# Dilated-attention mixer: the merge factors and the merge of a head pair moved to later visits, the fill of the last visit spread

## The chip, the cores and the metric

One core of one Trainium2 chip runs the whole program. The metric is the device time of one execution in microseconds (us), the median of 3 runs. All arithmetic is in 32-bit floats; products whose precision matters are made of three TensorE multiplications, with each operand split into a high and a low part.

## What is computed

A two-layer encoder on 512 tokens of width 1024. Each layer is a token mixer, a cross-attention into 256 memory tokens and a gated MLP, each followed by a residual and a layer norm. Layer 0 mixes by differential attention, layer 1 by dilated sliding-window attention. Only the mixer of layer 1 is touched:

```python
def dilated_attention(x, w_qkv, w_o):
    qkv = (x @ w_qkv).reshape(B, S, G, 3, H, E)          # G = 3 groups, H = 16 heads, E = 64
    for g, (window, dilation) in enumerate(((128, 1), (512, 4), (2048, 16))):
        o, l = dilated_group(qkv[:, :, g, 0], qkv[:, :, g, 1], qkv[:, :, g, 2], window, dilation, slopes)
        outs.append(o); lses.append(l)                   # output and log softmax denominator
    wts = softmax(stack(lses), axis=0)
    o = sum(wts[..., None] * stack(outs), axis=0)        # the merge
    return o.reshape(B, S, D) @ w_o
```

## The kernel before

**Pairs and visits.** `dil_attention` (line 643) works on 8 head pairs p = 0 to 7, each in two halves v = 0 and 1 of the queries. Its `main` (line 802) goes through visits i = 0 to 16. Visit i makes the scores of half i (pair i // 2, v = i % 2; line 713), turns the exponentials of half i - 1 by TensorE transposes in four sets k = 0 to 3 (line 767), and multiplies them with the values (`values`, line 772). So pair 6 is scored in visits 12 and 13 and has its values in visits 13 and 14; pair 7 is scored in visits 14 and 15 and has its values in visits 15 and 16; visit 16 scores nothing.

**One visit on the engines.** TensorE's 24 score matmuls fill four PSUM banks. VectorE adds the bias and finds the maximum (line 722, two instructions for each of four `u` tiles), ScalarE takes the exponential (line 724). A set of four transposes goes into one of two PSUM banks `ps_t` and is copied out into `PT` by line 769: sets 0 and 2 by VectorE (copy 0 and copy 2 below), sets 1 and 3 by ScalarE. `u` has four buffers: the scores of visit i write into the buffers that the turns of visit i set free. Set 2 needs the bank of set 0, so it waits for copy 0; the values wait for copies 2 and 3. At the end of `values` the result is copied out of PSUM into the tiles `O` (lines 786 to 790).

**Factors and merge.** The three groups of a pair are merged by their softmax denominators. `factors(p)` (line 731), called at the end of the scores of v = 1, sends the statistics through DRAM to change their layout (lines 737 to 741, POOL's DMA queue, into tile `x0`), works out the factors in nine small VectorE instructions and one on ScalarE (lines 747 to 756), and sends them through DRAM again, spread over the partitions, into tile `F` (lines 757 and 761, POOL's queue; one buffer). The merge, at the end of `values(p, 1)`, multiplies and adds the two `O` tiles (one buffer each) with `F` (lines 792 to 794, VectorE) and splits the sum into a high part (`o1h`, line 218, ScalarE) and a low part (`o1l`, line 219, VectorE) of the mixer's output, K-tile p of the product with `w_o`.

**What sets the order.** TensorE runs its instructions in the order in which they are written. VectorE, ScalarE and the DMA queues get theirs from a scheduler when the program is built: among the instructions that it holds to be ready, by its own estimate of times, the one written earlier goes first. Once built, each queue is strictly in order. `issue_after(ins)` puts an instruction somewhere behind `ins` in the queue of the same engine; it doesn't say how far behind.

**Fill.** `weave` (line 287) lets TensorE work on something else between the steps of a visit. Up to visit 13 that is the projection of the next pair (31 or 62 us of multiplications for two visits). For visits 14 to 16 only `on_.early(0)` is left: 12 triples of multiplications (a triple: lines 239, 240, 241) of the product with `w_o`, which need the K-tiles 0 to 5. `late = on_.early(1)` is another 12 triples; `take(late, t)` runs triples of it until t ns are used up, by 648 ns each. The code before takes 3 triples at the start of visit 16, 3 ahead of its values, and the remaining 6 behind them. Then `OutNorm.finish` (line 356) runs 8 triples of K-tiles 0 to 3 for the row blocks 2 and 3, and after these the triples of K-tiles 6 and 7, for row block 0 first. Their weights are loaded as `raw` and split into `whi` and `wlo` (lines 218 and 219).

Of the kernel before, what the change touches and what calls it, by code (L numbers as in the profile page):

```python
# [9 lines left out]
F32 = mybir.dt.float32  # L10
# [3 lines left out]
ALU = mybir.AluOpType  # L14
# [3 lines left out]
SEQ = 512  # L18
# [129 lines left out]
def encoder(ctx: ExitStack, tc: tile.TileContext, wall, xin, lam, subln, conv, lngb, tabf, tabd, eye, out):  # L148
    nc = tc.nc
# [130 lines left out]
    def take(gen, t):  # L280
        while t > 0:
            d = next(gen, None)
            if d is None:
                break
            t -= d
# [357 lines left out]
    def dil_attention(act, oT, pools, vp, ap, on_, led):  # L643
        tab = vp.tile([128, 768], F32, name="tabd")
        nc.scalar.dma_start(tab, tabd)
        NP = LH // 2
        qk, v0, v12, st0, st12, O = {}, {}, {}, {}, {}, {}


        def keys(x, b):  # L650
# [50 lines left out]
        def scores(p, v):  # L701
            (q0, k0, q1, k1, q2, k2) = qk[p]
            if v == 0:
                st0[p] = ap.tile([128, 4, 4], F32, tag="st0", name="st0")
                st12[p] = ap.tile([128, 4, 4], F32, tag="st12", name="st12")
            bs = 2 * v, 2 * v + 1
            Ss = {(b, c): psS.tile([128, 512], F32, tag="s", name="S") for b in bs for c in range(2)}
            for b in bs:
                for q_, k_, f in ((q0, keys(k0, b), slice(0, 256)), (q1, k1[:, b, :], slice(256, 384)),
                                  (q2, k2[:, b, :], slice(384, 512))):  # L710
                    for c in range(2):
                        h = sl(c, 64)
                        nc.tensor.matmul(Ss[b, c][:, f], q_[h, b, :], k_[h], start=True, stop=True)  # L713
            us = []
            for (b, c), S in Ss.items():
                u = ap.tile([128, 512], F32, tag="u", name="u", bufs=4)
                slope = 2.0 ** (-(2 * p + c + 1) / 2.0)
                for n, s in enumerate((st0[p], st12[p])):
                    f = sl(n, 256)
                    t = tab[:, 512:768] if n else tab[:, sl(b // 3, 256)]  # L720
                    m = s[:, b, 2 * c:2 * c + 1]
                    nc.vector.tensor_tensor_reduce(out=u[:, f], in0=S[:, f], in1=t, scale=-slope,  # L722
                                                   scalar=3.0e38, op0=ALU.add, op1=ALU.min, accum_out=m)
                    nc.scalar.activation(u[:, f], u[:, f], AF.Exp, bias=m, scale=-1.0,  # L724
                                         accum_out=s[:, b, 2 * c + 1:2 * c + 2])
                us.append(u)
            if v == 1:
                O[p] = [ap.tile([128, 512], F32, tag=f"O{n}", name="O", bufs=1) for n in range(2)], factors(p)
            return us

        def factors(p):

            eng = nc.gpsimd
            sd = dram.tile([SEQ, 4], F32, name=f"sd{p}")
            fd = dram.tile([2, 2, SEQ], F32, name=f"fd{p}")
            a, b = st0.pop(p), st12.pop(p)
            eng.dma_start(sd[64:448, :].rearrange("(b p) k -> p b k", p=128), a[:, 0:3, :])
            eng.dma_start(sd[448:512, :], a[0:64, 3, :])
            eng.dma_start(sd[0:64, :], a[64:128, 3, :])
            x = ap.tile([128, 4, 4], F32, tag="x0", name="x0")  # L740
            eng.dma_start(x, sd.rearrange("(k r) c -> k r c", r=4))

            ms = [t.rearrange("p r (c k) -> p k c r", k=2) for t in (x, b)]
            w = ap.tile([128, 2, 2, 4], F32, tag="w0", name="w0")
            e = ap.tile([128, 2, 2, 4], F32, tag="w1", name="w1")
            z = ap.tile([128, 2, 4], F32, tag="w2", name="w2")
            nc.vector.tensor_tensor(z, ms[0][:, 0], ms[1][:, 0], op=ALU.min)
            for n in range(2):
                nc.vector.tensor_tensor(w[:, :, n], z, ms[n][:, 0], op=ALU.subtract)
            nc.scalar.activation(e, w, AF.Exp)  # L750
            for n in range(2):
                nc.vector.tensor_tensor(w[:, :, n], e[:, :, n], ms[n][:, 1], op=ALU.mult)
            nc.vector.tensor_tensor(z, w[:, :, 0], w[:, :, 1], op=ALU.add)
            nc.vector.reciprocal(z, z)
            for n in range(2):
                nc.vector.tensor_tensor(w[:, :, n], e[:, :, n], z, op=ALU.mult)
            eng.dma_start(fd.rearrange("c s (k r) -> k c s r", r=4), w)
            F = ap.tile([128, 2, 512], F32, tag="F", name="F", bufs=1)
            for c in range(2):
                f = fd[c]  # L760
                eng.dma_start(F[sl(c, 64)], bass.AP(f.tensor, f.offset, [[0, 64], [SEQ, 2], [1, SEQ]]))
            return F

        def turn(u, n):
            tp = bank(pt, "t").rearrange("p (a b) -> p a b", b=128)
            for k in range(4):
                nc.tensor.transpose(tp[:, k, :], u[:, sl(k)], ident)  # L767
            PT = ap.tile([128, 4, 128], F32, tag="PT", name="PT", bufs=4)
            (nc.scalar.copy if n % 2 else nc.vector.tensor_copy)(PT, tp)
            return PT  # L770

        def values(p, v, PTs):
            o = bank(pt, "t")
            for x in range(2):
                b = 2 * v + x
                for n in range(4):
                    for c in range(2):
                        if n < 2:
                            V = v0[p // 2][b + n if b < 3 else 3 * n][:, (p % 2) * 128 + c * 64:]
                        else:  # L780
                            V = v12[p // 2][b][:, (p % 2) * 256 + (n - 2) * 128 + c * 64:]
                        nc.tensor.matmul(o[sl(c, 64), sl(2 * (n // 2) + x)], V[:, :64], PTs[2 * x + c][:, n, :],  # L782
                                         start=n % 2 == 0, stop=n % 2 == 1)
            (o0, o12), F = O[p]
            if v == 0:
                nc.scalar.copy(o0[:, 64:320], o[:, 0:256])
            else:
                nc.scalar.copy(o0[:, 320:512], o[:, 0:192])
                nc.scalar.copy(o0[:, 0:64], o[:, 192:256])
            nc.vector.tensor_copy(classes(o12)[:, sl(v, 2), :], o[:, 256:512].rearrange("p (r k) -> p r k", r=2))  # L790
            if v == 1:
                nc.vector.tensor_tensor(o0, o0, F[:, 0], op=ALU.mult)
                nc.vector.tensor_tensor(o12, o12, F[:, 1], op=ALU.mult)
                nc.vector.tensor_tensor(o0, o0, o12, op=ALU.add)
                evac(o0, oT[0][:, p, :], oT[1][:, p, :])

        def two_banks():
            return [psS.tile([128, 512], F32, tag="s", name="S") for _ in range(2)]
# [3 lines left out]
        def main():  # L802
            n = 2 * NP
            us = {}
            for i in range(n + 1):
                seg, step = (i // 2, 1 / 2.0) if i < n - 2 else (NP - 1, 1 / 3.0)
                pos = seg + (i - 2 * seg) * step
                yield pos
                if i < n:
                    us[i] = scores(i // 2, i % 2)  # L810
                else:
                    take(late, 1300)
                if i > 0:
                    PTs = []
                    for k in range(4):
                        yield pos + TURNS[k] * step
                        PTs.append(turn(us[i - 1][k], k))
                    yield pos + VALUES * step
                    if i == n:
                        take(late, 1300)  # L820
                    values((i - 1) // 2, (i - 1) % 2, PTs)

        run(proj(0))
        weave(main(), [(proj(p + 1), 6 * 5184 + 31104 * (p % 2)) for p in range(NP - 1)]
# [124 lines left out]
    for l in range(2):  # L949
        mt_kv = mems[l]  # L950
        oT = new_act(f"o{l}")
# [107 lines left out]
```

## Time and profile before

| what | us |
|---|---|
| median of 3 runs | 1894.35 |
| the three runs | 1894.87, 1894.35, 1891.37 |
| the profiled execution, its own time | 1890.71 |
| its span from first to last instruction | 1888.9 |
| TensorE busy in the span | 1863.5 (99%) |
| VectorE busy | 951.3 (50%) |
| ScalarE busy | 763.6 (40%) |
| POOL busy | 79.8 (4%) |

The profile is of one execution; its times count from the first instruction of the span. PE is TensorE's multiplications, PEld its weight loads, DVE is VectorE, ACT is ScalarE. In a row of the timeline stand the start, the duration, the engine, the line of the program, the operation, the tile written and the tiles read, shape and count; in square brackets, the idle time of the engine before it and what ended that. Successive instructions overlap a little at their ends. The dilated mixer lies between about 874 and 1320 us.

### The profile page before, as it was taken

The numbers are of one execution on the slowest core, as the hardware profiler recorded it, in microseconds if no ns is written. First come the engines' busy times: TensorE is split into PE (matmuls) and PEld (weight loads), VectorE is DVE, ScalarE is ACT, GpSimd is POOL, SyncE is SP. The second block draws the span as 40 slices with busy tenths as digits, with TensorE's granted clock in tenths as the row PEclk, the third lists the DMA queues.
The fourth block names the chain that finished last, engine by engine and source line by source line (L and its number), as shares of the span: only waits on it lengthen the run. The fifth ranks groups of instructions, "written<-read, shape, count | busy, mean of one in ns | idle before, by whom it ended". The sixth has DMA issues, their size and how long they took to land.

```text
span 1888.9 us, 25012 instructions
## 1 busy us (share of the span) xinstructions
PE 1863.5 (99%) x9896; PEld 1573.2 (83%) x9896; DVE 951.3 (50%) x1761; ACT 763.6 (40%) x1372; POOL 79.8 (4%) x116
## 2 busy tenths in 40 slices
PE   9999999999999999999999999999999999999998
PEld 7777788889888888899898898987888898888886
DVE  5578675547444432543444344445845564444324
ACT  4577654325333321333434344344534343333211
POOL 0011110000000000000000000001100000000000
PEclk9999999999999999999999999999999999999999
DMA  7121166234323324343223232231752343333241
GB/s 238 45 79 45 35 219 194 68 112 157 97 94 100 100 91 145 104 138 101 91 68 100 79 100 81 77 92 51 247 173 67 112 157 100 91 100 100 91 144 45
DMA packets 61573, 204.35 MB, mean 108 GB/s; under 512 B 8080, under 2 KB 8720, under 8 KB 61456
## 3 DMA queue, kind: packets, MB, share of 16 engines
q1 hardware_dynamic: 46080, 165.89, 27.8%
q10 hardware_dynamic: 12816, 32.47, 4.7%
q0 software_dynamic: 2560, 4.39, 1.1%
q8 instruction: 78, 1.28, 0.3%
q14 instruction: 39, 0.32, 0.1%
HBM read 190.01 MB, written 12.71 MB: 107 GB/s over the span
## 4 chain that ended last, share of the span: by engine, by line
PE 88%; DVE 5%; ACT 2%; DMA 2%; issue 1%; POOL 1%; DVEq 0%; POOLq 0%; ACTq 0%; SPq 0%
PE ps_a L239 16%; PE ps_a L240 16%; PE ps_a L241 16%; PE ps_o L239 7%; PE ps_o L241 7%; PE ps_o L240 7%; PE ps_s L241 2%; PE ps_s L240 2%; PE ps_s L239 2%; PE ps_t L241 2%; PE ps_t L239 2%; PE ps_t L240 2%; PE ps_t L782 2%; PE S L713 2%; PE ps_t L767 1%; ACT u L563 1%
## 5 line engine op out<-in xcount | busy, mean ns | idle before, releaser
L219 DVE TENSOR_TENSOR wlo<-raw,whi 128x1024 fp32r<-128x1024 f32 (+1 forms) x309 | 377.0, 1221 | 483.1 <-ACT whi L218 478.6
L218 ACT CAST whi<-raw 128x1024 fp32r<-128x1024 f32 (+1 forms) x309 | 323.7, 1049 | 583.6 <-PE ps_a L240 266.6
L239 PE MATMUL ps_a<-x2h,whi 128*128 128x512 f32 (+1 forms) x384 | 149.3, 389 | 0.0
L241 PE MATMUL ps_a<-x2h,wlo 128*128 128x512 f32 (+1 forms) x384 | 146.5, 381 | 0.0
L240 PE MATMUL ps_a<-x2l,whi 128*128 128x512 f32 (+1 forms) x384 | 146.3, 381 | 0.0
L239 PE MATMUL ps_a<-whi,x2h 128*128 128x512 f32 (+1 forms) x256 | 88.8, 347 | 0.0
L240 PE MATMUL ps_a<-wlo,x2h 128*128 128x512 f32 (+1 forms) x256 | 87.2, 341 | 0.0
L241 PE MATMUL ps_a<-whi,x2l 128*128 128x512 f32 (+1 forms) x256 | 87.2, 341 | 0.0
L241 PEld LDWEIGHTS ps_a<-x2h,wlo 128*128 128x128 f32 x384 | 72.2, 188 | 14.1
L239 PEld LDWEIGHTS ps_a<-x2h,whi 128*128 128x128 f32 x384 | 72.3, 188 | 14.0
L240 PEld LDWEIGHTS ps_a<-x2l,whi 128*128 128x128 f32 x384 | 72.3, 188 | 12.8
L724 ACT ACTIVATE u<-u,st 128x256 f32<-128x256 f32 x128 | 63.6, 498 | 38.4 <-DVE st L722 38.2
L239 PE MATMUL ps_o<-x1h,whi 128*128 128x512 f32 (+1 forms) x192 | 71.6, 373 | 0.0
L239 PE MATMUL ps_o<-x4h,whi 128*128 128x512 f32 (+1 forms) x192 | 71.6, 373 | 0.0
L240 PE MATMUL ps_a<-x1l,whi 128*128 128x512 f32 (+1 forms) x192 | 71.3, 371 | 0.0
L240 PE MATMUL ps_a<-x4l,whi 128*128 128x512 f32 (+1 forms) x192 | 71.3, 371 | 0.0
L239 PE MATMUL ps_a<-x1h,whi 128*128 128x512 f32 (+1 forms) x192 | 71.3, 371 | 0.0
L239 PE MATMUL ps_a<-x4h,whi 128*128 128x512 f32 (+1 forms) x192 | 71.3, 371 | 0.0
L241 PE MATMUL ps_a<-x1h,wlo 128*128 128x512 f32 (+1 forms) x192 | 71.3, 371 | 0.0
L241 PE MATMUL ps_a<-x4h,wlo 128*128 128x512 f32 (+1 forms) x192 | 71.3, 371 | 0.0
L241 PE MATMUL ps_o<-x1h,wlo 128*128 128x512 f32 (+1 forms) x192 | 71.3, 371 | 0.0
L241 PE MATMUL ps_o<-x4h,wlo 128*128 128x512 f32 (+1 forms) x192 | 71.3, 371 | 0.0
(420 smaller groups left out, 4447.4 us busy)
## 6 DMA issues: line engine op xcount, KB each, us to landing
raw<-in_wall_dram SPq DMA_DIRECT2D x314, 512.0 KB, 3.5
y<-row ACTq DMA_DIRECT2D x40, 256.0 KB, 3.0
row<-y ACTq DMA_DIRECT2D x20, 512.0 KB, 5.0
row<-in_lngb_dram ACTq DMA_DIRECT2D x12, 512.0 KB, 4.8
F<-fd POOLq DMA_DIRECT2D x16, 256.0 KB, 4.2
row<-in_x_dram ACTq DMA_DIRECT2D x4, 512.0 KB, 6.8
out_dram<-row ACTq DMA_DIRECT2D x8, 256.0 KB, 2.1
raw<-in_wall_dram ACTq DMA_DIRECT2D x2, 256.0 KB, 4.3
```

The source lines that it names most:

```text
L218: nc.scalar.copy(hi, ps)
L219: nc.vector.tensor_tensor(lo, ps, hi.bitcast(F32), op=ALU.subtract)
L239: nc.tensor.matmul(ps, ah, bh, start=start, stop=False)
L240: nc.tensor.matmul(ps, ah, bl, start=False, stop=False)
L241: nc.tensor.matmul(ps, al, bh, start=False, stop=stop)
L563: nc.scalar.activation(u, u, AF.Exp, bias=m, scale=-1.0, accum_out=sm[:, c:c + 1])
L713: nc.tensor.matmul(Ss[b, c][:, f], q_[h, b, :], k_[h], start=True, stop=True)
L724: nc.scalar.activation(u[:, f], u[:, f], AF.Exp, bias=m, scale=-1.0, accum_out=s[:, b, 2 * c + 1:2 * c + 2])
L767: nc.tensor.transpose(tp[:, k, :], u[:, sl(k)], ident)
L782: nc.tensor.matmul(o[sl(c, 64), sl(2 * (n // 2) + x)], V[:, :64], PTs[2 * x + c][:, n, :], start=n % 2 == 0, stop=n % 2 == 1)
```

## The change

`factors` is cut in two. Its first half, now `exchange(p)`, stays at the end of the scores of v = 1 (visit 2p + 1). Its second half, `factors(p)`, is called one visit later (visit 2p + 2), behind the four turns, and its first VectorE instruction is put behind copy 2 of that visit. The merge, now `merge(p)`, leaves `values` and is called one visit later (visit 2p + 3), behind the turns of set 1, its first VectorE instruction behind copy 0; for pair 7 it comes after the loop. Visit 16 takes `late` in other portions: 1900 ns ahead of set 0, 2600 ns ahead of set 2, 1300 ns ahead of the values. The `O` tiles are allocated in `values` of v = 0. `at[0]` is the last VectorE instruction of the scores or the turns.

```diff
@@ -644,7 +644,7 @@
         tab = vp.tile([128, 768], F32, name="tabd")
         nc.scalar.dma_start(tab, tabd)
         NP = LH // 2
-        qk, v0, v12, st0, st12, O = {}, {}, {}, {}, {}, {}
+        qk, v0, v12, st0, st12, O, X, Fs, at = {}, {}, {}, {}, {}, {}, {}, {}, {}
 
 
         def keys(x, b):
@@ -719,32 +719,40 @@
                     f = sl(n, 256)
                     t = tab[:, 512:768] if n else tab[:, sl(b // 3, 256)]
                     m = s[:, b, 2 * c:2 * c + 1]
-                    nc.vector.tensor_tensor_reduce(out=u[:, f], in0=S[:, f], in1=t, scale=-slope,
-                                                   scalar=3.0e38, op0=ALU.add, op1=ALU.min, accum_out=m)
+                    at[0] = nc.vector.tensor_tensor_reduce(out=u[:, f], in0=S[:, f], in1=t, scale=-slope,
+                                                           scalar=3.0e38, op0=ALU.add, op1=ALU.min, accum_out=m)
                     nc.scalar.activation(u[:, f], u[:, f], AF.Exp, bias=m, scale=-1.0,
                                          accum_out=s[:, b, 2 * c + 1:2 * c + 2])
                 us.append(u)
             if v == 1:
-                O[p] = [ap.tile([128, 512], F32, tag=f"O{n}", name="O", bufs=1) for n in range(2)], factors(p)
+                exchange(p)
             return us
 
-        def factors(p):
+        def exchange(p):
 
             eng = nc.gpsimd
             sd = dram.tile([SEQ, 4], F32, name=f"sd{p}")
-            fd = dram.tile([2, 2, SEQ], F32, name=f"fd{p}")
-            a, b = st0.pop(p), st12.pop(p)
+            a = st0.pop(p)
             eng.dma_start(sd[64:448, :].rearrange("(b p) k -> p b k", p=128), a[:, 0:3, :])
             eng.dma_start(sd[448:512, :], a[0:64, 3, :])
             eng.dma_start(sd[0:64, :], a[64:128, 3, :])
             x = ap.tile([128, 4, 4], F32, tag="x0", name="x0")
             eng.dma_start(x, sd.rearrange("(k r) c -> k r c", r=4))
+            X[p] = x
+
+        def factors(p):
+
+            eng = nc.gpsimd
+            fd = dram.tile([2, 2, SEQ], F32, name=f"fd{p}")
+            x, b = X.pop(p), st12.pop(p)
+            behind = tc.issue_after(at[0].ins)
 
             ms = [t.rearrange("p r (c k) -> p k c r", k=2) for t in (x, b)]
             w = ap.tile([128, 2, 2, 4], F32, tag="w0", name="w0")
             e = ap.tile([128, 2, 2, 4], F32, tag="w1", name="w1")
             z = ap.tile([128, 2, 4], F32, tag="w2", name="w2")
-            nc.vector.tensor_tensor(z, ms[0][:, 0], ms[1][:, 0], op=ALU.min)
+            with behind:
+                nc.vector.tensor_tensor(z, ms[0][:, 0], ms[1][:, 0], op=ALU.min)
             for n in range(2):
                 nc.vector.tensor_tensor(w[:, :, n], z, ms[n][:, 0], op=ALU.subtract)
             nc.scalar.activation(e, w, AF.Exp)
@@ -759,14 +767,17 @@
             for c in range(2):
                 f = fd[c]
                 eng.dma_start(F[sl(c, 64)], bass.AP(f.tensor, f.offset, [[0, 64], [SEQ, 2], [1, SEQ]]))
-            return F
+            Fs[p] = F
 
         def turn(u, n):
             tp = bank(pt, "t").rearrange("p (a b) -> p a b", b=128)
             for k in range(4):
                 nc.tensor.transpose(tp[:, k, :], u[:, sl(k)], ident)
             PT = ap.tile([128, 4, 128], F32, tag="PT", name="PT", bufs=4)
-            (nc.scalar.copy if n % 2 else nc.vector.tensor_copy)(PT, tp)
+            if n % 2:
+                nc.scalar.copy(PT, tp)
+            else:
+                at[0] = nc.vector.tensor_copy(PT, tp)
             return PT
 
         def values(p, v, PTs):
@@ -781,18 +792,23 @@
                             V = v12[p // 2][b][:, (p % 2) * 256 + (n - 2) * 128 + c * 64:]
                         nc.tensor.matmul(o[sl(c, 64), sl(2 * (n // 2) + x)], V[:, :64], PTs[2 * x + c][:, n, :],
                                          start=n % 2 == 0, stop=n % 2 == 1)
-            (o0, o12), F = O[p]
+            if v == 0:
+                O[p] = [ap.tile([128, 512], F32, tag=f"O{n}", name="O", bufs=1) for n in range(2)]
+            o0, o12 = O[p]
             if v == 0:
                 nc.scalar.copy(o0[:, 64:320], o[:, 0:256])
             else:
                 nc.scalar.copy(o0[:, 320:512], o[:, 0:192])
                 nc.scalar.copy(o0[:, 0:64], o[:, 192:256])
             nc.vector.tensor_copy(classes(o12)[:, sl(v, 2), :], o[:, 256:512].rearrange("p (r k) -> p r k", r=2))
-            if v == 1:
+
+        def merge(p):
+            (o0, o12), F = O.pop(p), Fs.pop(p)
+            with tc.issue_after(at[0].ins):
                 nc.vector.tensor_tensor(o0, o0, F[:, 0], op=ALU.mult)
-                nc.vector.tensor_tensor(o12, o12, F[:, 1], op=ALU.mult)
-                nc.vector.tensor_tensor(o0, o0, o12, op=ALU.add)
-                evac(o0, oT[0][:, p, :], oT[1][:, p, :])
+            nc.vector.tensor_tensor(o12, o12, F[:, 1], op=ALU.mult)
+            nc.vector.tensor_tensor(o0, o0, o12, op=ALU.add)
+            evac(o0, oT[0][:, p, :], oT[1][:, p, :])
 
         def two_banks():
             return [psS.tile([128, 512], F32, tag="s", name="S") for _ in range(2)]
@@ -808,17 +824,22 @@
                 yield pos
                 if i < n:
                     us[i] = scores(i // 2, i % 2)
-                else:
-                    take(late, 1300)
                 if i > 0:
                     PTs = []
                     for k in range(4):
                         yield pos + TURNS[k] * step
+                        if i == n:
+                            take(late, (1900, 0, 2600, 0)[k])
                         PTs.append(turn(us[i - 1][k], k))
+                        if k == 1 and i % 2 and i > 1:
+                            merge((i - 3) // 2)
+                    if i % 2 == 0:
+                        factors((i - 2) // 2)
                     yield pos + VALUES * step
                     if i == n:
                         take(late, 1300)
                     values((i - 1) // 2, (i - 1) % 2, PTs)
+            merge(NP - 1)
 
         run(proj(0))
         weave(main(), [(proj(p + 1), 6 * 5184 + 31104 * (p % 2)) for p in range(NP - 1)]
```

## Rows read from the trace of the kernel before

**Rows 1.** The page, part 1: engine, busy us, share of the span, instructions.
```profile
...
PE 1863.5 (99%) x9896; PEld 1573.2 (83%) x9896; DVE 951.3 (50%) x1761; ACT 763.6 (40%) x1372; POOL 79.8 (4%) x116
```

**Rows 2.** What TensorE waited for, 860 to 1320: us in total, times, longest.
```profile
...
PE ps_t L767 <- DVE PT L769: 1.8, 2, 1.4
PE ps_t L782 <- DVE PT L769: 1.7, 2, 0.9
```

**Rows 3.** Stretches: us, busy PE, PEld, DVE, ACT, POOL, clock, DMA share, GB/s.
```profile
...
880.00:1278.00 398.00, 398.00 (x2454) 349.54 (x2453) 174.13 (x415) 166.79 (x388) 26.50 (x43) 1.00 0.29 86
1278.00:1310.00 32.00, 27.65 (x239) 22.30 (x238) 17.32 (x63) 15.23 (x50) 5.92 (x10) 1.00 0.17 49
1310.00:1330.00 20.00, 20.00 (x116) 16.56 (x115) 8.05 (x15) 3.75 (x6) 1.83 (x3) 1.00 0.54 170
```

**Rows 4.** Timeline of visit 14: TensorE's turns and values (start, us, engine, line).
```profile
...
1287.80 0.63 PE L767 MATMUL ps_t<-ident,u 128*128 128x128 f32 x4 [0.43 <-DVE PT L769]
...
1291.20 1.97 PE L782 MATMUL ps_t<-PT,V 128*64 128x128 f32 x32 [0.86 <-DVE PT L769]
```

**Rows 5.** Timeline of visit 14 on VectorE.
```profile
...
1283.23 0.16 DVE L747 TENSOR_TENSOR w<-x,st 128x8 f32<-128x8 f32 x1
...
1285.58 0.42 DVE L722 CUSTOM_DVE_ANT_0 u<-S,tabd 128x256 f32<-128x256 f32 x1 [0.63 <-PE ps_t L767]
...
1290.37 0.69 DVE L769 COPY PT<-ps_t 128x512 f32<-128x512 f32 x1
```

**Rows 6.** Timeline of POOL's queue from visit 14 on.
```profile
...
1285.25 0.76 POOL L757 DMA_DIRECT2D fd<-w  x1 [3.55 <-DVE w L756]
...
1310.69 0.76 POOL L757 DMA_DIRECT2D fd<-w  x1 [3.70 <-DVE w L756]
```

**Rows 7.** Timeline of visit 15: TensorE.
```profile
...
1295.86 1.03 PE L767 MATMUL ps_t<-ident,u 128*128 128x128 f32 x8
...
1299.69 0.63 PE L767 MATMUL ps_t<-ident,u 128*128 128x128 f32 x4 [1.42 <-DVE PT L769]
...
1302.77 1.97 PE L782 MATMUL ps_t<-PT,V 128*64 128x128 f32 x32 [0.86 <-DVE PT L769]
```

**Rows 8.** Timeline of visit 15: VectorE, from the merge of pair 6 on.
```profile
...
1294.14 0.68 DVE L792 TENSOR_TENSOR O<-O,F 128x512 f32<-128x512 f32 x1
...
1296.88 0.69 DVE L219 TENSOR_TENSOR o1l<-O,o1h 128x512 fp32r<-128x512 f32 x1 [0.74 <-ACT o1h L218]
1297.49 0.42 DVE L722 CUSTOM_DVE_ANT_0 u<-S,tabd 128x256 f32<-128x256 f32 x1
```

**Rows 9.** Timeline of visit 16: TensorE.
```profile
...
1304.66 0.50 PE L239 MATMUL ps_a<-whi,o1h 128*128 128x512 f32 x1
...
1307.53 1.04 PE L767 MATMUL ps_t<-ident,u 128*128 128x128 f32 x8
```

**Rows 10.** Timeline behind visit 16: TensorE, the first products of the last K-tiles.
```profile
...
1325.07 0.39 PE L239 MATMUL ps_a<-whi,o1h 128*128 128x512 f32 x1
...
1325.75 0.39 PE L239 MATMUL ps_a<-whi,o1h 128*128 128x512 f32 x1
```

**Rows 11.** Timeline of visit 16 and behind it: VectorE.
```profile
...
1308.46 0.17 DVE L747 TENSOR_TENSOR w<-x,st 128x8 f32<-128x8 f32 x1 [2.61 <-DMA x<-sd]
...
1318.27 0.69 DVE L792 TENSOR_TENSOR O<-O,F 128x512 f32<-128x512 f32 x1 [1.66 <-DMA F<-fd]
...
1321.03 0.69 DVE L219 TENSOR_TENSOR o1l<-O,o1h 128x512 fp32r<-128x512 f32 x1 [0.74 <-ACT o1h L218]
1323.63 1.23 DVE L219 TENSOR_TENSOR wlo<-raw,whi 128x1024 fp32r<-128x1024 f32 x1 [1.92 <-ACT whi L218]
```

**Rows 12.** The same stretch: ScalarE.
```profile
...
1320.38 0.62 ACT L218 CAST o1h<-O 128x512 fp32r<-128x512 f32 x1 [4.41 <-DVE O L794]
```

**Rows 13.** Line 747's waits: us, times.
```profile
...
  DMA x<-sd: 9.9, 7
```

**Rows 14.** Tile F, its transfers from issue to landing.
```profile
...
DMA to landing us min/median/max: 3.4/4.2/6.7
```

## The prediction

> **What bounds the kernel now.** I read the page's busy times first: TensorE is busy for 1863.5 of 1888.9 us [rows 1], so a change to VectorE's queue can only give back time in which TensorE stands still. I then cut the mixer into stretches [rows 3]. From 880 to 1278, visits 1 to 13, TensorE is busy for 398.00 of 398.00 us: there the projection of the next pair covers every wait, and whatever VectorE does earlier or later costs and gives nothing. From 1278 to 1310, visits 14 to 16, it is busy for 27.65 of 32.00: 4.35 us are lost, all that the mixer has to give. From 1310 to 1330 it is full again, 20.00 of 20.00. The granted clock is 1.00 (2.4 GHz) in all three, also in the one with the gaps, so the clock is no term.
>
> The list of TensorE's waits names what it waits for [rows 2]: the copies of line 769 on VectorE, 3.5 us in four waits; the rest of the 4.35 are ScalarE's copies. The timeline places them. In visit 14 set 2 waits 0.43 and the values 0.86 [rows 4]; in visit 15 set 2 waits 1.42 and the values 0.86 [rows 7]; visit 16 has none. The two visits do the same work, so the difference of 1.42 and 0.43 is what something extra does in visit 15.
>
> **The change part by part.** Durations are from the profiled execution, 1890.71 us with a span of 1888.9; the median of the runs shown, 1894.35, is 3.64 above it. I add the sum to the median.
>
> *Merge out of visit 14's values: a gain.* Now the merge of pair 6 starts at 1294.14, its last instruction (o1l) runs from 1296.88 to 1297.57, and only then comes the first line 722 of visit 15, at 1297.49 [rows 8]. In visit 14, where nothing stands ahead of it, line 722 had waited for TensorE's turn [rows 5]; a set of four transposes takes 0.63 [rows 4], so in visit 15, with the turns at 1295.86 [rows 7], it could start at 1296.49, 1.00 earlier. Visit 14 gives what follows: line 722 at 1285.58, copy 2 at 1290.37 (4.79 later) [rows 5], values at 1291.20 (5.62 later) [rows 4]. So visit 15 would have copy 2 at 1301.28 and its values at 1302.11, not 1302.77: a gain of 0.66, less than the 1.00 because the later steps of visit 15 already run a little closer together.
>
> *Factors out of visit 13 (pair 6).* They were no stall: line 722 of visit 14 came after them and waited for TensorE all the same [rows 5]. Visit 14 keeps its waits. In steady state line 747 has waited for its transfer 9.9 us in seven of eight visits [rows 13]; that ends, and is worth nothing, since TensorE was covered there.
>
> *The merge in visit 15: a new wait.* The factors of pair 6 now start behind copy 2 of visit 14, which ends at 1291.06 [rows 5]. From line 747 to the first transfer (line 757) it takes 2.02 (1283.23 to 1285.25) [rows 5, 6], and from line 757 to a merge that had waited for F, 7.58 (1310.69 to 1318.27) [rows 6, 11]. So F lands at about 1300.7. The binding only puts the merge somewhere behind copy 0 of visit 15 (about 1298.6). It is written ahead of sets 2 and 3, so when it and copy 2 can both run, the merge goes first. Copy 2 could run at 1301.28, when F has landed: the three VectorE instructions of the merge (2.1 from line 792 to the cast of o1h [rows 11, 12], 2.0 on VectorE) go ahead of it. Copy 2 moves to 1303.3, the values to 1304.1, against 1302.77 now: a loss of 1.3 in place of the gain of 0.66. The bounds: -0.66 if copy 2 is ahead of the merge, +2.1 if the merge stands right behind copy 0 and holds VectorE until F lands (below). I take +1.3, the order that the program's text gives with the transfer at its measured length. Behind the merge nothing else is late: the `O` tiles are wanted again only by the copies behind the values. In POOL's queue the F of pair 6 (issued at about 1296) still goes ahead of the statistics of pair 7.
>
> *Factors of pair 7, and the spread fill: a second new wait.* Now line 747 runs at 1308.46, as soon as its transfer lands [rows 11]. Afterwards it stands behind copy 2 of visit 16, and the fill puts 5 more triples ahead of set 2 in place of none. The first triple of visit 16 starts at 1304.66, sets 0 and 1 at 1307.53 [rows 9]; a triple takes 0.68 (1325.07 to 1325.75) [rows 10]. Sets 0 and 1 take some 0.8 of TensorE; 2 triples of the fill and 5 of `late` make 4.8. So set 2 starts at 1313.2, copy 2 runs from 1313.9 to 1314.5, line 757 follows 2.02 later, at 1316.5, and F lands 7.58 later, at 1324.1, 5.8 after the 1318.27 of now. From the start of the merge to the end of the cast of o1h it takes 2.73 (1318.27 to 1321.00), to the end of o1l 3.45 (1321.72) [rows 11, 12]: 1326.8 and 1327.5. TensorE wants o1h of K-tile 7 at 1325.75 and o1l 0.45 later [rows 10]; the number of triples ahead of that is unchanged. So it waits 1.1 for the one and 0.3 more for the other: 1.4. VectorE must also split the weights of K-tiles 6 and 7, 1.23 from 1323.63 on [rows 11], for a triple that starts at 1325.07: whichever of the two goes first, the other is later by 0.75 or more, so up to 2.15. I take 1.75, between the two; below 0 nothing, as there is no wait to gain here [rows 3], and above 3.0 if both weight splits go ahead of o1l. If visit 15 ends earlier or later, all of this moves with it.
>
> *The rest of the spread.* Visit 16 has no wait that 3 or 5 triples ahead of its sets could fill: 0. Later `late` triples behind the values covered the chain of pair 7; that price is in the 1.75.
>
> **Sum.** +1.3 +1.75 = +3.05, from 1894.35: 1897.4.
>
> **The rivals.**
> A, copy 2 first. If the scheduler holds F to land later than 1301.28, copy 2 goes ahead of the merge in visit 15 and the gain of 0.66 stays. Against it: seven waits of line 747 [rows 13] show an order drawn up with transfers shorter than they are. -0.66 + 1.75 = +1.1: 1895.5.
> B, the forecast.
> C, the merge as a plug (slower than before). With a transfer estimated 2 us short, the merge stands right behind copy 0 of visit 15, and VectorE waits for F from 1298.6 to 1300.7 with four line 722 and copy 2 behind it: 1300.7 + 2.0 + 1.4 puts copy 2 at 1304.1 and the values at 1304.9, +2.1; with o1l ahead of copy 2 too, +2.8. With 1.75 that is +3.85 to +4.55: 1898.6. It decides when the estimate puts F before the line 722 of set 2 (about 1299.3). For it: [rows 13]; against it, those waits are only 1.4 each.
> D, F comes sooner. With the shortest landing of F, 3.4 and not 4.2 [rows 14], and no weight split in the way, the wait of K-tile 7 falls to 0.6; with half a microsecond less again, to nothing, and A's gain remains: 1893.7.
> The Trainium skill, page "DMA: Bandwidth & Descriptors", section on the anatomy of one DMA on the software path, puts such a transfer at about 2.0 us plus its bytes at 436 GB/s; for 8 KB and 256 KB that would be an estimated 4.6 us where the rows have 7.58, and then D would hold with no wait at all. The trace does not agree: the two transfers and their issue took the 7.58.
> E, nothing is left of the waits (or, as small, the order on VectorE doesn't change at all and the time stays). All 4.35 gone is 1890.0; but 1.29 of it at least (0.43 and 0.86 [rows 4]) is visit 14's, which no part touches.
>
> **How the numbers follow.** About 0.2% (3.8 us: below 1890.6, above 1898.1) is what a measurement of this kernel can tell from no change. Chances: A 0.22, B 0.42, C 0.20, D 0.10, E 0.06. The forecast's own term sizes run from +2.0 to +4.3. Slower by over 0.2%: 0.11 of B, 0.14 of C, 0.01 of A: 0.26. Faster: 0.04 of E, 0.03 of D if the median falls among the lower runs: 0.07. The rest, 0.67, is within 0.2%. Range: down to 1891.5 (D and the lower runs), up to 1899.5 (C, without its worst).
>
> **What would show it.** Right: TensorE idle for 1 to 3 us some 20 us behind the values of visit 15, released by o1h, o1l or a weight split; line 747 of pair 7 some 6 us later than now; in visit 15 the wait of set 2 down from 1.42 to about 0.4, and the wait of the values up from 0.86 to about 3 with the merge ahead of copy 2. Wrong: copy 2 ahead of the merge (A); line 792 with an idle time for F in visit 15 (C); no wait at K-tile 7 (D). The forecast fails at large if TensorE has waits between 880 and 1278, or if those of visit 14 go.

## The result, and the profile after

| what | before | after |
|---|---|---|
| median, us | 1892.16 (6 runs, 1890.23 to 1894.87) | 1900.69 (6 runs, 1898.27 to 1903.99) |
| the profiled execution, us | 1890.71 | 1900.63 |
| its span, us | 1888.9 | 1898.8 |

The ratio of after to before is 1.0044, 95% interval [1.0034, 1.0054]: 8.5 us slower. The forecast was 1897.4 in a range up to 1899.5, so the sign of its sum held and its size did not: +3.05 were foreseen, +8.5 came. (The forecast was added to 1894.35, the median of three runs; the six have 1892.16.) The two profiled executions stand 9.9 us apart, and the steps below are accounted between them.

Line numbers moved by 8 to 16. After, the factors begin at line 755 (747 before), their two transfers are lines 765 and 769 (757 and 761), the turns are 775 (767), VectorE's copies of `PT` 780 (769), the values 793 (782), the merge 808 to 810 (792 to 794). First the page's busy times and the stretches of after (columns as in [rows 1] and [rows 3]).

```profile
PE 1870.3 (98%) x9896; PEld 1577.6 (83%) x9896; DVE 951.7 (50%) x1761; ACT 762.8 (40%) x1372; POOL 79.0 (4%) x116
```

```profile
880.00:1278.00 398.00, 398.00 (x2454) 349.53 (x2453) 174.55 (x415) 166.49 (x388) 26.52 (x44) 1.00 0.29 86
1278.00:1310.00 32.00, 26.44 (x225) 21.48 (x223) 15.84 (x54) 13.90 (x46) 5.88 (x10) 0.95 0.16 42
1310.00:1330.00 20.00, 18.32 (x110) 14.59 (x108) 6.99 (x17) 4.50 (x8) 1.83 (x3) 1.00 0.16 41
1330.00:1350.00 20.00, 16.73 (x63) 13.04 (x64) 10.52 (x24) 5.22 (x8) 0.56 (x1) 0.85 0.58 222
...
1303.50:1307.00 3.50, 3.47 (x33) 3.33 (x34) 1.17 (x2) 0.99 (x3) 0.70 (x2) 0.59 0.03 5
1330.00:1334.00 4.00, 3.90 (x9) 2.72 (x10) 1.07 (x2) 0.04 (x1) 0.00 (x0) 0.57 0.68 240
...
1334.00:1340.00 6.00, 6.00 (x28) 4.94 (x27) 0.10 (x1) 0.00 (x0) 0.00 (x0) 1.00 1.01 402
...
1346.00:1351.00 5.00, 4.79 (x18) 4.02 (x19) 5.00 (x9) 2.31 (x4) 0.32 (x1) 0.66 0.35 111
```

Visits 1 to 13 are as full as before [rows 3]: the moved merges and factors cost nothing where a projection covers them. The loss begins at 1278. Two things are new against [rows 1, 3]: idle time in stretches that had none, and a clock below 1.00. TensorE is *busy* for 6.8 us more with the same 9896 instructions (1.7 of it lie in the first 400 us, where it idles 1.7 less). In two short stretches the granted clock is 0.59 and 0.57: most of each ran at the lower of its two levels (0.50 of full speed, 1.2 GHz), called half clock below. Over the whole span the six runs of after have a granted clock of 0.995 to 0.997, and the runs of before beside the experiments 0.997 to 0.999, so it isn't the profiled execution alone. TensorE's three longest waits from 1278 to 1400 (us in total, times, longest) say for what it stood still:

```profile
PE ps_t L793 <- DVE PT L780: 3.3, 1, 3.3
PE ps_a L432 <- DVE row L426: 3.2, 1, 3.2
PE ps_a L239 <- ACT o1h L218: 1.3, 1, 1.3
```

One is at the values of visit 15, one at K-tile 7, and one that no part of the prediction names, at the transposes of row block 0 (line 432), which follow its layer norm. Here are these places on TensorE's timeline of after:

```profile
1297.95 0.63 PE L775 MATMUL ps_t<-ident,u 128*128 128x128 f32 x4 [0.43 <-DVE PT L780]
...
1303.53 3.34 PE L793 MATMUL ps_t<-PT,V 128*64 128x128 f32 x32 [3.32 <-DVE PT L780]
1306.80 0.50 PE L239 MATMUL ps_a<-whi,o1h 128*128 128x512 f32 x1
...
1327.20 0.39 PE L239 MATMUL ps_a<-whi,o1h 128*128 128x512 f32 x1
1328.06 0.50 PE L240 MATMUL ps_a<-wlo,o1h 128*128 128x512 f32 x1 [0.47 <-DVE wlo L219]
...
1330.10 0.67 PE L239 MATMUL ps_a<-whi,o1h 128*128 128x512 f32 x1 [1.30 <-ACT o1h L218]
...
1334.01 0.39 PE L239 MATMUL ps_a<-whi,o1h 128*128 128x512 f32 x1
...
1346.21 0.66 PE L432 MATMUL ps_a<-ident,row 128*128 128x128 f32 x4 [3.17 <-DVE row L426]
...
1350.82 0.40 PE L239 MATMUL ps_t<-whi,o1h 128*128 128x512 f32 x1
```

The two steps of before that answer to the last two of these, and that no row ahead shows:

```profile
1336.63 0.60 PE L432 MATMUL ps_a<-ident,row 128*128 128x128 f32 x4
...
1339.58 0.39 PE L239 MATMUL ps_t<-whi,o1h 128*128 128x512 f32 x1
```

Subtracting the start of the same step before from its start after gives how far after is behind, and each difference between neighbours is what the stretch between them cost:

| step of TensorE | before | after | behind by | this stretch |
|---|---|---|---|---|
| set 2 of visit 14 | 1287.80 | 1287.37 | -0.43 | arose ahead of the visits |
| values of visit 14 | 1291.20 | 1290.44 | -0.76 | -0.33: the wait for ScalarE's copy of set 1, ahead of set 3, fell from 0.55 to 0.22 |
| set 2 of visit 15 | 1299.69 | 1297.95 | -1.74 | -0.98: its wait fell from 1.42 to 0.43 |
| values of visit 15 | 1302.77 | 1303.53 | +0.76 | +2.50: the wait of 3.32 |
| start of visit 16 | 1304.66 | 1306.80 | +2.14 | +1.38: the values at half clock, 3.27 instead of 1.89 |
| K-tile 6 | 1325.07 | 1327.20 | +2.13 | 0 |
| K-tile 7 | 1325.75 | 1330.10 | +4.35 | +2.22: waits of 0.47 and 1.30; the other 0.45 is overlap lost at the waits (multiplications of 0.39 that elsewhere start 0.23 apart) |
| transposes of row block 0 | 1336.63 | 1346.21 | +9.58 | +5.23: +1.87 at half clock up to 1334.01, then the wait of 3.17 |
| next products | 1339.58 | 1350.82 | +11.24 | +1.66: half clock again (0.66 from 1346 to 1351) |
| end of the span | 1888.9 | 1898.8 | +9.9 | -1.3: later waits are shorter |

(1.87 is 1334.01 - 1330.10 = 3.91 for three triples, less three times the 0.68 of [rows 10]. The rest of 5.23, 3.36, goes with the wait of 3.17.) The half clock takes 1.38 + 1.87 + 1.66 = 4.9 us of it, in this one execution; how long it lasts differs from run to run, as the experiments show.

**Why each wait is there.** VectorE in visit 15, from copy 0 (1297.12) to copy 2 (1302.70), between which before had nothing but its line 722:

```profile
1297.12 0.69 DVE L780 COPY PT<-ps_t 128x512 f32<-128x512 f32 x1
1300.11 0.69 DVE L808 TENSOR_TENSOR O<-O,F 128x512 f32<-128x512 f32 x1 [2.31 <-DMA F<-fd]
1300.72 0.42 DVE L722 CUSTOM_DVE_ANT_0 u<-S,tabd 128x256 f32<-128x256 f32 x1
...
1302.10 0.69 DVE L809 TENSOR_TENSOR O<-O,F 128x512 f32<-128x512 f32 x1
1302.70 0.68 DVE L780 COPY PT<-ps_t 128x512 f32<-128x512 f32 x1
```

The merge's first instruction stands right behind copy 0 and waits 2.31 for `F`, with line 722 and copy 2 queued behind it. `F` is late because the factors of pair 6 were bound behind copy 2 of visit 14. POOL's queue, with the first VectorE instructions of pair 7's factors and merge:

```profile
1292.52 0.77 POOL L765 DMA_DIRECT2D fd<-w  x1 [11.24 <-DVE w L764]
1295.60 1.07 POOL L769 DMA_DIRECT2D F<-fd  x2 [2.31 <-DMA fd<-w]
...
1318.58 0.77 POOL L765 DMA_DIRECT2D fd<-w  x1 [10.94 <-DVE w L764]
```

```profile
1316.58 0.16 DVE L755 TENSOR_TENSOR w<-x,st 128x8 f32<-128x8 f32 x1
...
1326.18 0.69 DVE L808 TENSOR_TENSOR O<-O,F 128x512 f32<-128x512 f32 x1 [4.03 <-DMA F<-fd]
```

From line 765 to a merge that waits for `F` it takes 7.59 for pair 6 (1292.52 to 1300.11) and 7.60 for pair 7 (1318.58 to 1326.18), as the 7.58 of before [rows 6, 11]. Last, ScalarE's queue behind the mixer, and the instruction of VectorE that uses the loaded rows; ACTq rows are DMA issues:

```profile
1329.43 0.62 ACT L218 CAST o1h<-O 128x512 fp32r<-128x512 f32 x1 [0.98 <-DVE O L810]
1329.58 0.97 ACTq L366 DMA_DIRECT2D row<-in_lngb_dram  x2
1330.75 3.85 ACTq L371 DMA_DIRECT2D row<-y  x4
```

```profile
1339.90 0.69 DVE L414 SCALAR_TENSOR_TENSOR row<-row,ps_a 128x512 f32<-128x512 f32 x1 [8.82 <-DMA row<-y]
```

The same issues before:

```profile
1322.55 0.33 ACTq L371 DMA_DIRECT2D row<-y  x1
...
1325.43 1.30 ACTq L371 DMA_DIRECT2D row<-y  x3
```

Line 371 loads the residual rows that row block 0's layer norm adds. Its issues stand in ScalarE's queue behind the cast of `o1h`, which waits for the merge of pair 7. The cast went from 1320.38 [rows 12] to 1329.43, so the first load went from 1322.55 to 1330.75, and VectorE stood 8.82 us for it. The Trainium skill, page "DMA: Bandwidth & Descriptors", section "Anatomy of one DMA — SWDGE (gpsimd) path", says that a transfer waits for a semaphore only in the issuing sequencer, before it is dispatched. For POOL's queue the trace of experiment e4 agrees: there the issue of two loads stands for 6.96 us, until `o1l` is written. On ScalarE's queue the issues of line 366 start 0.15 us behind the start of the cast in both kernels (1320.53 and 1329.58), and those of line 371 follow them.

### The profile page after: what moved, and what is told of

Read it like the earlier page. It is cut to its first block, busy times and chain, and to the rows that moved or that the text cites. A ratio compares the mean times of both kernels' runs of the same rounds, so it can differ in the third digit from the quotient of the medians.

```text
span 1898.8 us, 25020 instructions
## 1 busy us (share of the span) xinstructions
PE 1870.3 (98%) x9896; PEld 1577.6 (83%) x9896; DVE 951.7 (50%) x1761; ACT 762.8 (40%) x1372; POOL 79.0 (4%) x116
```

## The experiments

Ten kernels, each timed beside the kernel before on the same chip. Its medians there are 1892.1 us (e1 to e4), 1891.88 (e5 to e8) and 1893.1 (e9 and e10), and its single runs spread from 1888.7 to 1896.5. The differences in us below are between medians; the ratio and its 95% interval are of the runs. The first four take one suspected loss each out of the changed kernel.

**e1: Merge behind copy 2, all three instructions bound.** If the plug is the order on VectorE, it and the half clock behind it go together.

```diff
             with tc.issue_after(at[0].ins):
                 nc.vector.tensor_tensor(o0, o0, F[:, 0], op=ALU.mult)
-            nc.vector.tensor_tensor(o12, o12, F[:, 1], op=ALU.mult)
-            nc.vector.tensor_tensor(o0, o0, o12, op=ALU.add)
+                nc.vector.tensor_tensor(o12, o12, F[:, 1], op=ALU.mult)
+                nc.vector.tensor_tensor(o0, o0, o12, op=ALU.add)
...
-                        if k == 1 and i % 2 and i > 1:
+                        if k == 3 and i % 2 and i > 1:
```

> The changed kernel with all three VectorE instructions of the merge (not the first alone) behind copy 2 of their visit. Theory (three separate waits: the merge of pair 6 holds VectorE for F in visit 15; K-tile 7 comes late; the residual rows are loaded late; each followed by a stretch at half clock): the wait of the values in visit 15 falls from 3.3 to about 0.9 us, no stretch at half clock follows it, and 2.5 + 1.4 = 3.9 us of the 8.5 go: about +4.6 us against the kernel before. The waits behind visit 16 stay as they are. Rival (the last pair's factors alone set the end of the mixer, so that time won in visit 15 is waited for later): the wait of K-tile 7 grows by what visit 15 wins, and the time stays at about +8.5.

Measured: 1896.9, ratio 1.0021 [1.0011, 1.0031], +4.8 in place of +8.5. The values of visit 15 on its timeline:

```profile
1303.10 1.97 PE L793 MATMUL ps_t<-PT,V 128*64 128x128 f32 x32 [0.88 <-DVE PT L780]
```

The wait is 0.88 for 3.32, and the 32 multiplications take 1.97 for 3.34: without the long wait, no half clock there. The waits at K-tile 7 (1.30) and at row block 0 (2.39) stay; the first is followed by half clock (0.50 from 1330 to 1332), the second isn't (1.00 from 1344 to 1350). The plug and what follows from it are some 3.7 of the 8.5 (the two differences were measured on different occasions, here and below).

**e2: The last fill as before.**

```diff
+                else:
+                    take(late, 1300)
...
-                        if i == n:
-                            take(late, (1900, 0, 2600, 0)[k])
```

> The changed kernel with the old portions of the late triples (3 at the start of visit 16, 3 ahead of its values, 6 behind). Theory: copy 2 of visit 16, the factors of pair 7 and F come 3.4 us earlier, so the wait of K-tile 7 (1.3 and 0.5 us, and the half clock after it, 1.9) goes; the residual rows are issued some 3 us earlier, which shortens the wait of the transposes of row block 0 (3.2, and 1.7 of half clock) but may not end it. Visit 15 stays as it is. About +3 to +5 us against the kernel before. Rival (the spread of the fill is harmless, the move of the factors alone is at fault): +8.5.

Measured: 1895.24, 1.0013 [1.0003, 1.0023], +3.1. No wait for `o1h` is left; the values of visit 15 wait 3.56, row block 0 waits 2.13, with half clock behind both. (The profiled execution was this kernel's slowest, 1899.47, so only single waits are read from it.)

**e3: The factors of pair 7 early.** They are called right behind `exchange(7)` and not bound; all else stays as changed.

```diff
                 exchange(p)
+                if p == NP - 1:
+                    factors(p)
...
-            behind = tc.issue_after(at[0].ins)
+            behind = tc.issue_after(at[0].ins) if p < NP - 1 else ExitStack()
...
-                    if i % 2 == 0:
+                    if i % 2 == 0 and i < n:
                         factors((i - 2) // 2)
```

> The changed kernel with the factors of pair 7 alone called at once behind its exchange, in visit 15, unbound, as in the kernel before. Theory: both waits behind visit 16 go (K-tile 7 and the late residual rows) with their stretches at half clock; what stays is visit 15 (2.9 us at the start of visit 16): about +2.5 us against the kernel before. Rival (the merge call behind the loop, or the spread fill, delays K-tile 7 or the rows by itself): a wait of over 1 us stays behind visit 16 and the time is +5 or more.

Measured: 1894.7, 1.0011 [1.0002, 1.0021], +2.6. No wait for `o1h`, only 0.77 at row block 0, and still 3.46 at the values of visit 15. This run and the one before reach the end of the mixer from two sides, with fewer triples ahead of pair 7's copy 2 or with factors that don't wait for it. They save 5.4 and 5.9 us of the 8.5, more than the wait at K-tile 7 (2.22): without it there is no half clock behind K-tile 7, and the rows come sooner after the start of visit 16 (28.4 us in e2 and 27.2 in e3, against 33.1 after).

**e4: The residual rows on POOL's queue.** Only the DMA issues of lines 366 and 371 change engine.

```diff
+                eng = nc.gpsimd if ln == 3 else nc.scalar
...
-                    nc.scalar.dma_start(xs[q], res[sl(q), :])
+                    eng.dma_start(xs[q], res[sl(q), :])
```

> The changed kernel with the loads of scale, shift and residual rows of the norm behind the mixer issued from POOL's queue and not from ScalarE's. Theory (they are late because ScalarE's queue holds them behind the cast of o1h of pair 7, which waits for the merge): they start before 1325 us, the wait of 3.2 us for row block 0 goes with its stretch at half clock, 3 to 4.9 us less: +4 to +5.5 against the kernel before. Rival (they wait for the buffers of the merge's tiles O and F, which they take over): they start no earlier than the end of the merge and the time stays at about +8.5.

Measured: 1896.71, 1.0024 [1.0015, 1.0034], +4.6. TensorE no longer waits at row block 0; the 3.59 of visit 15 and the 1.30 at K-tile 7 stay. So the late rows and their half clock are some 3.9. POOL's queue shows what the order does now:

```profile
1324.33 1.11 POOL L372 DMA_DIRECT2D row<-y  x2
1332.39 1.10 POOL L372 DMA_DIRECT2D row<-y  x2 [6.96 <-DVE o1l L219]
```

The first two loads leave 6 us ahead of the cast of `o1h` (1330.45 in this run); the other two wait for `o1l` even so, so for these the rival holds.

**e5: Both repairs together**, the bound merge and the early last factors.

> Experiments 1 and 3 together: the whole merge behind copy 2, and the factors of pair 7 called at once in visit 15. Theory (the waits are separate and add up): +2.6 of experiment 3 less the 3.7 that experiment 1 took off makes -1.1 us against the kernel before; of TensorE's waits in visits 14 to 16 those of about 1.5 us a visit stay, and one of about 0.8 us for row block 0 behind them. Rival (the waits hide one another, so that the second repair finds nothing left): 0 to +2.6.

Measured: 1889.04, 0.9985 [0.9976, 0.9994], 2.8 us *faster* than before, more than the 1.1 that was expected, though the interval reaches down to 1.1. From 1278 to 1380 the clock is 1.00 throughout, and TensorE's longest wait is 0.9.

**e6: the same with the rows on POOL's queue as well.**

> Experiment 5 with the rows of the norm behind the mixer loaded from POOL's queue as in experiment 4. Theory: the remaining wait of 0.8 us for row block 0 goes too: about -1.9 us against the kernel before. Rival (the transposes then wait for VectorE instead): as experiment 5, -1.1.

Measured: 1889.05, 0.9982 [0.9973, 0.999]: not to be told from the one without, since there the rows are hardly late.

**e7: The new portions of the fill alone**, in the kernel before.

> The kernel before with nothing changed but the portions of the late triples (3 ahead of set 0, 5 ahead of set 2, 3 ahead of the values of visit 16). Theory: with the factors of pair 7 where they were, F lands at the same time and the portions move no wait: 0 us, at most 1 either way, against the kernel before, and no wait for o1h at K-tile 7. Rival (the portions alone make K-tile 7 late): +2 or more, with a wait for o1h.

Measured: 1890.16, 0.9993 [0.9984, 1.0002]: no loss, and no wait for `o1h`. (Its profiled execution, its slowest with 1894.28, waits 1.48 at row block 0.) The spread by itself is harmless. It costs only together with factors bound behind copy 2 of visit 16, which it moves back.

**e8: The fill of visits 14 and 15 put where TensorE waits**, on top of both repairs and the rows on POOL: the twelve triples of `early(0)` are laid out as 1 ahead of sets 0 and 1, 3 ahead of sets 2 and 3, 2 ahead of the values.

```diff
-                        yield pos + TURNS[k] * step
+                        yield pos + (TURNS if i < n - 2 else (0.15, 0.15, 0.66, 0.66))[k] * step
...
-              + [(on_.early(0, lambda: [bank(pa, "a") for _ in range(2)]), 7776, 0.0)], LEAD)
+              + [(on_.early(0, lambda: [bank(pa, "a") for _ in range(2)]), 11664, 0.0)], LEAD)
```

> Experiment 6 with the 12 triples of the last fill all in visits 14 and 15, in each 1 ahead of set 0, 3 ahead of set 2 and 2 ahead of the values (before: 1, 2 and 1, and 4 in visit 16). Theory: the waits of 0.43 and 0.86 us left in both visits are filled with work, 2.6 us, and set 3 waits a little less: -4 to -5 us against the kernel before, with the granted clock at 1.00 from 1278 to 1340. Rival (the chain of pair 7, from its exchange to o1h, takes over, since K-tile 7 is now wanted 2.8 us earlier): a wait for o1h at K-tile 7 takes back what the visits win, -1 to -2 us.

Measured: 1886.97 (1885.23 to 1887.59), 0.9971 [0.996, 0.9983], 4.9 us faster than before: this version beats both kernels, and its slowest run is below the fastest of before. Its stretch of the last visits:

```profile
1278.00:1310.00 32.00, 31.25 (x256) 25.69 (x255) 20.62 (x69) 15.73 (x51) 6.66 (x11) 1.00 0.16 47
```

31.25 of 32 are busy, where before had 27.65 [rows 3].

**e9: The same fill in the kernel before**, with merge and factors where they were.

> The kernel before, with only the last fill put elsewhere: of the twelve fill triples of visits 14 and 15, the portions that run ahead of the waiting transposes and ahead of the values are made larger and the one at the visit's start smaller; merge and factors stay where they were. Theory: the gain of e8 over e5 is the fill standing in the waits, and needs no moved merge: the waits of 0.43 and 0.86 us of visits 14 and 15 go, the 1.42 of visit 15 (merge of pair 6 still ahead of the fill's own copies there) shrinks or goes too, so 1.5 to 2.7 us of 1892, i.e. about 1889.8 (ratio 0.9986 to 0.9992). Rival: what e8 won came from the merge's later place (bound on all three operations), and the fill alone gives nothing: 1892 +- 1, with the waits before sets 2 and the values of visits 14 and 15 still at 0.4 to 1.4.

Measured: 1889.58, 0.9985 [0.9974, 0.9996], 3.5 below the median of before. Waits that were 1.42 and 0.86 [rows 7] on its timeline:

```profile
1299.74 0.63 PE L767 MATMUL ps_t<-ident,u 128*128 128x128 f32 x4 [0.72 <-DVE PT L769]
...
1302.82 1.97 PE L782 MATMUL ps_t<-PT,V 128*64 128x128 f32 x32 [0.17 <-DVE PT L769]
```

The fill needs no moved merge to gain. Whether the repaired move adds to it is not settled: the intervals of this run and of the one before it overlap, and they ran on different chips.

**e10: The changed kernel without the binding of the factors.** One instruction loses its constraint; the later calls, the bound merge and the new portions stay.

```diff
-            behind = tc.issue_after(at[0].ins)
...
-            with behind:
-                nc.vector.tensor_tensor(z, ms[0][:, 0], ms[1][:, 0], op=ALU.min)
+            nc.vector.tensor_tensor(z, ms[0][:, 0], ms[1][:, 0], op=ALU.min)
```

> The changed kernel with the binding of the factors' first operation taken off; the later calls, the binding of the merge's first operation and the new portions stay. Theory: the loss comes from the binding of the factors, which makes F's transfer of pair 6 start 7.6 us ahead of a merge that stands directly behind copy 0, and in visit 16 puts pair 7's factors ahead of the last fill's copies. Without it F lands early: no plug of 2.3 us behind copy 0 in visit 15, so the values of visit 15 wait for 1.2 us or less and not 3.3, no half clock there, and K-tile 7 waits for no cast. That leaves the kernel before within 1.5 us (1890.5 to 1893.5) or, if the residual rows still come late, +1.5. Rival: the loss comes from the merge's later place itself, and stays over +4 us (1896 or more), with the 3.3 us wait of visit 15 there as before.

Measured: 1890.16, 0.9985 [0.9975, 0.9994]: 2.9 below before, and 11.5 less than the changed kernel's +8.5 (each against its own runs of before). VectorE and TensorE in its visit 15 (the merge is lines 806 to 808 here, the factors begin at line 753):

```profile
1284.25 0.17 DVE L753 TENSOR_TENSOR w<-x,st 128x8 f32<-128x8 f32 x1
...
1295.02 0.69 DVE L807 TENSOR_TENSOR O<-O,F 128x512 f32<-128x512 f32 x1
1297.19 0.42 DVE L722 CUSTOM_DVE_ANT_0 u<-S,tabd 128x256 f32<-128x256 f32 x1 [1.48 <-PE ps_t L773]
...
1299.18 0.68 DVE L806 TENSOR_TENSOR O<-O,F 128x512 f32<-128x512 f32 x1
```

```profile
1303.15 1.97 PE L791 MATMUL ps_t<-PT,V 128*64 128x128 f32 x32 [1.46 <-DVE PT L778]
```

The factors of pair 6 run ahead of line 722 of visit 14 again, `F` is there before the merge, and the bound multiplication (line 806) follows copy 0 without a wait for it. The values wait 1.46, a little over the 1.2 that was expected, because the whole merge still goes ahead of copy 2. No wait at K-tile 7 is left. So the loss is the binding of the factors: it made both transfers of `F` start late. The merge's later place alone costs nothing that shows. (The binding of pair 6's factors was not taken off by itself; e3 does that for pair 7's.)

What stays open: between the profiled executions, this kernel gains nothing from 1278 to 1340 (57.53 us busy, against 57.65 before) and 2.1 from 1340 to 1400 (59.38 against 57.27). Why the stretch behind the mixer is fuller in it was not tried.

## Why the prediction was wrong

In short: the forecast's two terms came to 3.4 us (1.19 in visits 14 and 15, 2.22 at K-tile 7) in place of 3.05. What failed are two things that it put at nothing: the clock (4.9 us) and whatever comes behind K-tile 7 (3.4 us).

**The reading of the bound held.** Nothing moved between 880 and 1278, and all of the loss begins at visit 14.

**The factors of pair 6: right.** `F` was forecast at about 1300.7; the merge started on it at 1300.11, which with the 0.43 that after was ahead is 1300.54. The 7.58 of before carried over (7.59). The 2.02 became 2.31 (line 755 at 1290.21, line 765 at 1292.52), which the earlier end of copy 2 in visit 14 nearly made up for.

**The merge in visit 15: case C took place, not B.** The step that failed here is "when it and copy 2 can both run, the merge goes first", which set the merge at the moment when `F` lands. The scheduler had put its first instruction right behind copy 0, so VectorE waited 2.31 (C said 2.1). The size hardly suffered, by luck: two instructions of the merge, not three, went ahead of copy 2, and visit 14 gave back 0.33 that the forecast had not counted, so the values came 1.19 us later than before once the 0.43 is taken out (0.76 + 0.43), where B had +1.3. The first multiplication alone was bound, and it made the trouble; the run with all three behind copy 2 shows it.

**"The clock is no term": wrong, and the largest miss, 4.9 us.** It was read from a profile whose longest wait in the mixer was 1.42 [rows 3, 7]. The forecast itself made longer ones (values "up from 0.86 to about 3") and carried the old clock over to them. The run with the bound merge shows the link: with 0.88 in place of 3.32, the values take 1.97 again.

**K-tile 7: right.** +1.75 was taken, between 1.1 and 2.15; 2.22 came, of which 1.77 are waits, for a weight split (0.47) and `o1h` (1.30), as forecast. `F` of pair 7 landed at 1326.18, 2.08 behind the forecast 1324.1, and visit 16 had begun 2.14 later than before. The text had said that all of this moves with the end of visit 15.

**Nothing behind K-tile 7: wrong, 3.4 us and 1.7 of the half clock.** The step on pair 7 ends with TensorE's wait for `o1h` and `o1l`, and puts all that follows at nothing without a reason. (That "behind the merge nothing else is late" is said of pair 6 only, and there no wait contradicts it.) It left out what stands in ScalarE's queue behind the cast of `o1h`: four loads of residual rows, due at row block 0's norm. Before, their place behind the cast cost nothing, since the cast was early. With the rows on POOL's queue the wait is gone.

**The rivals.** D relied on a shorter chain of transfers. The Trainium skill, page "DMA: Bandwidth & Descriptors", section "Anatomy of one DMA — SWDGE (gpsimd) path", would give an estimated 4.6 us for it; 7.59 and 7.60 came, so the measurement decides against it. In the trace of after, pair 7's 8 KB land 2.2 us after their issue and the 256 KB 4.1, where the page gives an estimated 2.0 and 2.6. In size none of the rivals came near +8.5, for all used one clock and ended at K-tile 7. C, the nearest with its 1898.6, lacked the same two terms.

Summed anew: -0.33 - 0.98 + 2.50 (visits 14 and 15), +2.22 (K-tile 7), +3.36 (rows) and +4.91 (half clock) make 11.7; the later waits give back 1.3, and after was 0.43 ahead before all this: 9.9, the distance of the two spans.

## What to carry to other kernels

A constraint that holds an instruction back also holds back the transfer that it feeds: before binding one, add the measured time from it to the consumer (here 2.0 and 7.6 us) and see what stands in the consumer's strictly ordered queue. When a cast moves by 9 us, list the DMA issues behind it in its engine's queue, not only the readers of its result. And when a forecast makes a wait longer than any in the profile, the clock read from that profile no longer covers it.

## What the runs showed of the hardware that was not expected

- **The clock after waits.** TensorE is 98 to 99% busy in these kernels, and yet one wait of 3.32 us was followed by 3.3 us at a granted 0.59, and in three other runs waits of 3.46 to 3.59 stretched the same 32 multiplications from 1.97 to 2.62, 2.92 and 3.68. Single waits of 1.42 (before [rows 7]), 1.46 (e10) and 1.54 (e9) were followed by none, with 1.00 in their stretches. Two short waits near each other, 0.47 and 1.30, were followed by 4 us at 0.57 in the changed kernel. In between, the length of a wait doesn't settle it: at row block 0 one of 2.39 (e1) was followed by 1.00, and one of 2.13 (e2) by 3 us at 0.50. What decides it there, no run shows.
- **The cost of a late load.** From its first issue to the instruction that had waited for it, the load of row block 0's rows took 9.15 us (1330.75 to 1339.90), where the page has 5.5 as the median of such a load from issue to landing. From 1330 to 1334 the DMA engines were 0.68 busy at 240 GB/s, and from 1334 to 1340 full (1.01) at 402 GB/s. Two weight loads (issued from 1328.04 on), the two loads of line 366 and the four of line 371, each of 512 KB, were under way together, and all four of line 371 landed 9.1 to 9.8 us after their issue. At 402 GB/s these 4.2 MB are an estimated 10.4 us. So the loads seem to have held one another up; no run tests it.
